# Encoder block on one core: weight norms two jobs ahead, table loads spread over a job, four eviction buffers, three transpose banks

## The chip, the cores and the metric

The program runs on one core of a Trainium2 chip. The metric is the device time of one launch in microseconds (us); for the kernel before it is the median of three runs. Everything about the program's inside comes from one profiled execution of it.

The core's engines have a queue of instructions each, which they work off in order: PE (TensorE) multiplies matrices into PSUM, DVE (VectorE) and ACT (ScalarE) do element-wise work, POOL (GpSimd) too, and SP (SyncE) issues nearly all DMAs of the stages told of here. Engines meet through semaphores. PSUM has eight banks of 128 x 512 fp32.

## The reference

One encoder layer on 2048 tokens of width 1024, in fp32. Cut to what matters here:

```python
h = rmsnorm(x, g_attn_norm)
proj = h @ w_in                       # 1024 -> 1952
q_a, k_a, v_a, c_q, c_kv, k_rope = split(proj, [512, 512, 512, 256, 128, 32])
out_a = mixer_dilated(q_a, k_a, v_a, rel_bias)   # 8 heads of 64, windows (128,1), (512,4), (2048,16)
out_b = mixer_mla(c_q, c_kv, k_rope, ...)        # latent attention
x = x + concat(rmsnorm(out_a), rmsnorm(out_b)) @ w_out
x = x + hierarchical_moe(rmsnorm(x), ...)
return rmsnorm(x, g_final)
```

`mixer_dilated` adds to every score a bias that depends on the distance of key and query (`rel_bias` through a bucket table).

## The kernel before

The code is scheduled by hand: on every engine the instructions stand in the order in which the Python code emits them. A projection in fp32 accuracy is made of three fp16 products: each operand is split into `hi` and `lo` (ACT writes `hi`, DVE the remainder `lo`), and 24 matmuls (8 blocks of the inner dimension x hi*hi, hi*lo, lo*hi) build one output tile. The scale of a split is a power of two taken from a norm of the weights: `pow2_scale` sums the squares over the partitions with a tiny matmul of ones (L375, called p2 below) and makes the power of two with some ten DVE instructions.

**The x stage** (0 to 150 us) runs over the 16 blocks of 128 tokens, c = 0 to 15. `stage_a` loads and normalises a block, `stage_b` transposes it on PE (L167, two tiles of one PSUM bank each from pool `pt`) and splits it out of PSUM (ACT L102, DVE L103) into `hT`, `stage_c` makes the latent projection of a block (24 matmuls of 416 columns, L176). Between them generators emit side work, a step for each c: `tables` makes the bias tables (pairs of matmuls L462/L463 into pool `tb`, copied out by DVE at L464, two banks), `vb_scale` and `vscale` take norms with p2 matmuls into `pt`.

**The jobs** (150 to 435 us): two "v" jobs of 16 chunks (24 matmuls of 256 columns, L336), then four "qk" jobs of 8 chunks (24 matmuls of 512 columns, L354). `jobs[i]` runs out of split weights; while it runs, the weights of job i+1 are split and those of job i+2 are fetched. At the start of job i, ahead of its first matmul, stands `qkscale(i + 1)`: an ACT square of the whole raw weight (`qk_junk`, L268), then two p2 matmuls. A chunk's PSUM tile (pool `pm`, four banks) is evicted by ACT L364 and DVE L365 into `qk_sb` (two buffers of each half), and SP stores both (L367). From job 2 on a generator `v_copies` (`vc`) makes SP issue DRAM-to-DRAM copies of v (`d_v`, `d_v1e`, `d_v4e`) after a chunk's matmuls, ahead of its store.

**The last job** runs two further things: `pre3` at its start loads what phase 3 needs first (`QA`, `KA`, `KB`, and the bias tables: `t16` in one DMA, `t1` in sixteen pieces, L500), and `ahead3` issues, one step for each chunk, five loads of v (L508) and then four pieces of the table `t4` (L518).

**Phase 3** is the dilated attention, head by head: S matmuls (L681/L682), bias added by POOL (`pp`, L723/L729), exponent by ACT and so on. POOL scales each bias table in place once (L614): `t16`, then `t1`, which needs all sixteen pieces; the first `pp` stands behind it.

The lines that set the order around a job:

```python
for i, (kind, g) in enumerate(jobs):
    if i == len(jobs) - 1:
        self.pre3(); a3 = self.ahead3()
    if i + 1 < len(jobs):
        if jobs[i + 1][0] == "qk":
            for _ in qkscale(i + 1): pass
        split_job(i + 1)
    if i + 2 < len(jobs): fetch(i + 2)
    # chunks: 24 matmuls; next(vc); next(a3); evict; store
```

## Time and profile before

| what | value |
| --- | --- |
| median of three runs | 2306.95 us (2306.91 to 2308.32) |
| the profiled execution's own time | 2312.83 us |
| its span, first to last instruction | 2310.6 us |
| mean granted TensorE clock | 0.953 |
| busy: PE | 2060.5 us (89% of the span) |
| busy: DVE, ACT, POOL | 1666.5 (72%), 1439.9 (62%), 1092.7 us (47%) |

The span is what the rows of the trace add up to; the profiled execution took 5.9 us more than the median run. A busy share is a mean over stages: PE is close to full over the whole, so what counts is where it stands idle and what it then waits for. A row of a timeline gives start and length in us, engine, line, operation, `out<-in`, shapes, how many instructions were run together, and in brackets the idle time just before with what ended it.

### The profile page before, as it was taken

To read this page: it belongs to the slowest core of one execution; us is meant where nothing else is said; L and a number is where in the kernel's file an instruction comes from. 1 tells how busy PE (TensorE), PEld (TensorE's weight loads), DVE (VectorE), ACT (ScalarE), POOL (GpSimd) and SP (SyncE) were. 2 spreads that over 40 slices of the span, in tenths; PEclk is the share of its full clock that TensorE was granted. 3 is DMA by queue.
4 is the path that set the end of the run, shared out by engine and by line. 5 is a ranking of instruction groups with operands and counts; after the bars stand their busy time and mean duration, and the time that the engine had idled before them with its cause. 6 is when DMAs were issued, how large, how long until landed. Compare 5 with 4: busy or idle time off the path is not lost. (4 is left out here: it accounts for less than half of the span.)

```text
span 2310.6 us, 42905 instructions
## 1 busy us (share of the span) xinstructions
PE 2060.5 (89%) x16099; PEld 1458.3 (63%) x16099; DVE 1666.5 (72%) x3741; ACT 1439.9 (62%) x2125; POOL 1092.7 (47%) x1193
## 2 busy tenths in 40 slices
PE   5889989788889899999999999898888899999990
PEld 3458434577778466665655655577776588788870
DVE  7732221488887788888888899968787577777765
ACT  5532211499997588888888878744343366667653
POOL 1110000377763255555555556644654656667740
PEclk9989989999999899999999999899998999999995
DMA  4412344956735100000000221154444789999978
GB/s 153 131 54 68 123 151 122 224 139 153 163 100 154 37 20 22 6 22 21 7 22 9 55 93 24 34 165 143 150 147 147 219 298 293 291 308 319 311 211 308
DMA packets 196676, 312.81 MB, mean 135 GB/s; under 512 B 64185, under 2 KB 149090, under 8 KB 183460
## 3 DMA queue, kind: packets, MB, share of 16 engines
q1 hardware_dynamic: 166420, 174.43, 26.4%
q0 software_dynamic: 29760, 134.85, 18.2%
q8 instruction: 127, 2.08, 0.4%
q14 instruction: 81, 0.66, 0.1%
q10 hardware_dynamic: 288, 0.79, 0.1%
HBM read 235.66 MB, written 101.25 MB: 146 GB/s over the span
## 5 line engine op out<-in xcount | busy, mean ns | idle before, releaser
L961 POOL TENSOR_TENSOR lo<-p,hi 128x512 f16<-128x512 f32 x256 | 343.0, 1344 | 295.5 <-ACT p L955 233.7
L954 ACT ACTIVATE hi<-S,mla_scale 128x1024 f16<-128x1024 f32 x256 | 285.5, 1115 | 135.0 <-PE S L949 133.4
L923 DVE TENSOR_REDUCE part<-M 128x1 f32<-128x512 f32 x512 | 340.4, 680 | 13.1 <-PE M L921 11.7
L955 ACT ACTIVATE p<-S,mla_scale 128x1024 f32<-128x1024 f32 x256 | 285.2, 1114 | 0.0
L960 DVE TENSOR_TENSOR lo<-p,hi 128x512 f16<-128x512 f32 x256 | 228.9, 895 | 12.1 <-ACT p L955 10.3
L983 PE MATMUL O<-VB,lo 128*128 128x65 f16 x2048 | 198.9, 194 | 6.8 <-DVE lo L960 4.3
L978 PEld LDWEIGHTS <-hi 128*128 128x128 f16 x2048 | 184.9, 98 | 27.0 <-issue 21.5
L978 PE MATMUL O<-VB,hi 128*128 128x129 f16 (+1 forms) x2048 | 198.9, 215 | 0.0
L983 PEld LDWEIGHTS <-lo 128*128 128x128 f16 x2048 | 177.7, 99 | 17.4 <-DVE lo L960 5.9
L729 POOL TENSOR_TENSOR pp<-sb,st 128x256 f32<-128x256 f32 (+1 forms) x256 | 142.9, 581 | 45.1 <-DVE st L706 32.9
L2117 DVE TENSOR_TENSOR s<-raw,s 128x1024 fp32r<-128x1024 f32 x120 | 140.2, 1221 | 17.1 <-ACT s L2115 16.0
L1425 PE MATMUL pm<-s,mT_hi 128*128 128x512 f32 x512 | 137.3, 415 | 3.8 <-ACT mT_hi L1410 3.8
L2074 PE MATMUL pd<-s,hT 128*128 128x512 f32 x540 | 138.2, 404 | 1.7 <-ACT hT L2061 1.7
L614 POOL TENSOR_SCALAR t<-t,a_scale 128x512 f32<-128x512 f32 (+1 forms) x12 | 16.1, 1354 | 261.3 <-DMA t<-d_r 245.2
L2161 POOL DMA_INDIRECT d_x<-o,rec x47 | 88.1, 1874 | 106.7 <-ACT s L2115 33.7
L365 DVE SCALAR_TENSOR_TENSOR qk_sb<-pm,wscale,qk_sb 128x512 f16<-128x512 f32 x32 | 24.0, 750 | 149.3 <-ACT qk_sb L364 149.3
L746 PE MATMUL PT<-ident,pp 128*128 128x128 f32 (+1 forms) x640 | 104.5, 287 | 25.6 <-ACT pp L733 24.0
L2115 ACT ACTIVATE s<-raw 128x1024 fp32r<-128x1024 f32 x120 | 118.2, 1049 | 12.8 <-DMA raw<-in_w_up,eidx 6.8
L733 ACT ACTIVATE pp<-pp,a_scale 128x512 f32<-128x512 f32 (+1 forms) x160 | 114.0, 713 | 11.2 <-POOL pp L729 9.5
L2074 PEld LDWEIGHTS pd<-s,hT 128*128 128x128 f32 x540 | 101.2, 188 | 30.1 <-issue 4.3
L364 ACT ACTIVATE qk_sb<-pm,wscale 128x512 f16<-128x512 f32 x32 | 22.0, 688 | 153.4 <-DMA d_qk<-qk_sb 76.8
L1425 PEld LDWEIGHTS pm<-s,mT_hi 128*128 128x128 f32 x512 | 98.8, 198 | 26.1 <-ACT mT_hi L1410 4.1
(511 smaller groups left out, 5963.7 us busy)
## 6 DMA issues: line engine op xcount, KB each, us to landing
x<-in_x SPq DMA_DIRECT2D x32, 512.0 KB
na<-d_na SPq DMA_DIRECT2D x48, 264.0 KB
d_qk<-qk_sb SPq DMA_DIRECT2D x64, 128.0 KB
d_x<-x SPq DMA_DIRECT2D x16, 512.0 KB
d_h<-h SPq DMA_DIRECT2D x16, 512.0 KB
y<-d_x SPq DMA_DIRECT2D x16, 512.0 KB
out<-y SPq DMA_DIRECT2D x16, 512.0 KB
d_q<-qs SPq DMA_DIRECT2D x16, 384.0 KB
```

Of the source, the lines that this page charges most:

```text
L729: nc.gpsimd.tensor_sub(dst, src, res[:, s0 + i, 65:66, None, None].to_broadcast([128, 2, na, nx // 2]))
L923: nc.vector.tensor_reduce(part[m][:, qt, kc:kc + 1], ps, axis=AX.X, op=ALU.max)
L954: nc.scalar.activation(hi, ps, AF.Exp, scale=es)
L955: nc.scalar.activation(p32, ps, AF.Exp, scale=es)
L960: nc.vector.tensor_sub(lo[:, :, 0:LV], p32[:, :, 0:LV], hi[:, :, 0:LV])
L961: nc.gpsimd.tensor_sub(lo[:, :, LV:512], p32[:, :, LV:512], hi[:, :, LV:512])
L978: nc.tensor.matmul(o[:, c0:c0 + own], hi[:, j, q], V[:, 0:own], start=(kt == 0 and qt == 0), stop=False, skip_group_check=True)
L983: nc.tensor.matmul(o[:, c0:c0 + 65], lo[:, j, q], V[:, 0:65], start=False, stop=(kt == 15 and qt == 3), skip_group_check=True)
L1425: nc.tensor.matmul(ps[half], mT[a][:, j], wo[b][j // 2][:, j % 2, 512 * half:512 * half + 512], start=(n == 0), stop=(n == 23))
L2074: self.nc.tensor.matmul(ps[:, half], hT[a][:, j], w[b][:, j, 512 * half:512 * half + 512], start=(n == 0), stop=(n == len(k) - 1))
L2115: nc.scalar.activation(hi, src, AF.Copy)
L2117: eng.tensor_sub(lo, src, hi)
```

## The change

- `wscale` and `qkscale` get a tile for each use (6 and 4 instead of 3 and 2).
- `pt` (transposes) gets a third PSUM bank, `pm` (projections) goes from four to three. In the x stage the p2 matmuls of `vb_scale` and `vscale` write into pool `tb`, whose two banks the tables use, instead of `pt`.
- `qkscale(i + 2)` runs in steps inside job i: in v jobs one step after the matmuls of each chunk from 8 on, in qk jobs two steps after each chunk from 4 on. `qkscale(i + 1)` at the job's start is gone.
- `qk_sb` gets four buffers instead of two.
- The sixteen `t1` loads leave `pre3`. `ahead3` issues two of them after each v load and ahead of each `t4` piece.

```diff
-            wsc = [hp.tile([128, 3], F32, name=f"wscale{i}") for i in range(3)]
-            sq = [hp.tile([128, 2], F32, name=f"qkscale{i}") for i in range(2)]
+            wsc = [hp.tile([128, 3], F32, name=f"wscale{i}") for i in range(6)]
+            sq = [hp.tile([128, 2], F32, name=f"qkscale{i}") for i in range(4)]
...
+            norms = []
...
-                yield from self.pow2_scale(sm, pt, am, 1.0, w[:, 0:1], None, w[:, 1:2])
+                yield from self.pow2_scale(sm, norms[0], am, 1.0, w[:, 0:1], None, w[:, 1:2])
...
-            pt = ctx.enter_context(tc.tile_pool(name="p1pt", bufs=2, space=PSUM))
-            pm = ctx.enter_context(tc.tile_pool(name="p1pm", bufs=4, space=PSUM))
+            pt = ctx.enter_context(tc.tile_pool(name="p1pt", bufs=3, space=PSUM))
+            pm = ctx.enter_context(tc.tile_pool(name="p1pm", bufs=3, space=PSUM))
...
-                yield from self.pow2_scale(sm, pt, am, float(D), vsc, dr["va_inv"])
+                yield from self.pow2_scale(sm, norms[0], am, float(D), vsc, dr["va_inv"])
...
                 nc.scalar.activation(jk, raws[i], AF.Square, accum_out=am[:, 0:1])
                 nc.vector.tensor_copy(am[:, 2:3], gmax)
-                s2 = sq[g % 2]
+                yield
+                s2 = sq[g]
...
             tb = c1.enter_context(tc.tile_pool(name="p1tb", bufs=2, space=PSUM))
+            norms[0] = tb
             tables = self.bias_tables(rawp, xp.tile([128, 4, 768], F32R, name="onehot", bufs=1), tb)
-            vb = self.vb_scale(rawp, pt, sm)
+            vb = self.vb_scale(rawp, tb, sm)
...
                 if c == NT - 1:
                     c1.close()
+                    norms[0] = pt
...
-                    if jobs[i + 1][0] == "qk":
-                        for _ in qkscale(i + 1):
-                            pass
                     split_job(i + 1)
+                steps = iter(())
                 if i + 2 < len(jobs):
                     fetch(i + 2)
+                    steps = qkscale(i + 2)
...
+                        if c >= 8:
+                            next(steps, None)
                         vt = vts[c % 2]
...
-                            s2 = wsc[g % 2 + 1][:, 2:3]
-                            qs = [qkp.tile([128, 512], F16, name=f"qk_sb{t}") for t in range(2)]
+                            if 4 * hh + n4 >= 4:
+                                next(steps, None)
+                                next(steps, None)
+                            s2 = wsc[g + 1][:, 2:3]
+                            qs = [qkp.tile([128, 512], F16, name=f"qk_sb{t}", bufs=4) for t in range(2)]
...
-        for c in range(16):
-            nc.sync.dma_start(self.t1[8 * c:8 * c + 8], AP(dr["t1"], (15 - c) * 16, [[496, 8], [8 * 496, 8], [1, 256]]))
...
+        def table1(c0):
+            for c in range(2 * c0, 2 * c0 + 2):
+                nc.sync.dma_start(self.t1[8 * c:8 * c + 8], AP(dr["t1"], (15 - c) * 16, [[496, 8], [8 * 496, 8], [1, 256]]))
...
-        yield from self.load_v(0, self.v_first)
+        for i, _ in enumerate(self.load_v(0, self.v_first)):
+            table1(i)
+            yield
         for a in range(4):
+            table1(4 + a)
             nc.sync.dma_start(self.t4[32 * a:32 * a + 32].rearrange("p h (a x) -> p (h a) x", a=4),
                               AP(dr["r4"], a * 3072, [[1, 32], [96, 32], [1, 64]]))
             yield
```

Three places show how the instructions stand. First ACT at the boundary from job 3 to job 4, before: evictions of job 3 (`qk_sb`, L364), then `qk_junk`, the square of the weights of job 5, and `wc_hi`, the split of those weights (the bracket names the semaphores that the instruction waits for, by engine or DMA queue):

```order
L364 ACTIVATE qk_sb_2828<-pm,wscale_114 128x512 [waits DMAHW0_49,DVE_49,PE_49]
L364 ACTIVATE qk_sb_2861<-pm,wscale_114 128x512 [waits DMAHW4_49,DVE_49,PE_49]
L364 ACTIVATE qk_sb_2894<-pm,wscale_114 128x512 [waits DMAHW0_49,DVE_49,PE_49]
L364 ACTIVATE qk_sb_2927<-pm,wscale_114 128x512 [waits DMAHW4_49,DVE_49,PE_49]
L364 ACTIVATE qk_sb_2959<-pm,wscale_114 128x512 [waits DMAHW0_49,DVE_49,PE_49]
L364 ACTIVATE qk_sb_2991<-pm,wscale_114 128x512 [waits DMAHW4_49,DVE_49,PE_49]
L268 ACTIVATE qk_junk,vmax<-raw 128x2048 [waits DMAHW5_49]
L102 ACTIVATE wc_hi<-raw,wscale_114 128x16x64 [waits DVE_49]
L102 ACTIVATE wc_hi<-raw,wscale_114 128x16x64
```

and with the change, all eight evictions of job 3 (L374), with the same weights' square and split:

```order
L374 ACTIVATE qk_sb_2767<-pm,wscale_114 128x512 [waits DMAHW2_49,PE_49,Activation_49]
L374 ACTIVATE qk_sb_2800<-pm,wscale_114 128x512 [waits DMAHW5_49,PE_49,Activation_49]
L374 ACTIVATE qk_sb_2833<-pm,wscale_114 128x512 [waits DMAHW7_49,DVE_49,PE_49]
L374 ACTIVATE qk_sb_2866<-pm,wscale_114 128x512 [waits DMAHW2_49,DVE_49,PE_49]
L271 ACTIVATE qk_junk,vmax<-raw 128x2048 [waits DMAHW5_49,DMAHW4_49]
L374 ACTIVATE qk_sb_2909<-pm,wscale_114 128x512 [waits DMAHW0_49,DVE_49,PE_49]
L374 ACTIVATE qk_sb_2956<-pm,wscale_114 128x512 [waits DMAHW4_49,DVE_49,PE_49]
L374 ACTIVATE qk_sb_3001<-pm,wscale_114 128x512 [waits DMAHW0_49,DVE_49,PE_49]
L374 ACTIVATE qk_sb_3033<-pm,wscale_114 128x512 [waits DMAHW4_49,DVE_49,PE_49]
L102 ACTIVATE wc_hi<-raw,wscale_116 128x16x64 [waits DVE_49]
L102 ACTIVATE wc_hi<-raw,wscale_116 128x16x64
```

The square has moved from the boundary up into the middle of job 3, behind the fourth of its evictions, so four evictions lie between it and the split that needs its norm.

Next SP at the start of the last job. `QA` to `KB` and `t_3300` (t16) are loaded by `pre3`, `t_3301` is t1, `v` the loads of `ahead3`, `d_qk<-qk_sb` the stores of chunks. Before:

```order
L367 DMA d_qk<-qk_sb_3283 128x512
L560 DMA QA_3302<-d_qk 64x2048 x2
L564 DMA KA<-d_qk 64x2048 x2
L564 DMA KB<-d_qk 64x2048 x2
L498 DMA t_3300<-d_r_67 128x8x128
L500 DMA t_3301<-d_t_65 8x8x256 x16
L508 DMA v_3353<-d_va 128x16x260
L367 DMA d_qk<-qk_sb_3355 128x512
L367 DMA d_qk<-qk_sb_3356 128x512
L508 DMA v_3353<-d_v_59 128x15x260
L508 DMA v_3353<-d_v1e 96x4x260
L367 DMA d_qk<-qk_sb_3388 128x512
```

and with the change (`t_3306` is t1):

```order
L377 DMA d_qk<-qk_sb_3288 128x512
L575 DMA QA_3307<-d_qk 64x2048 x2
L579 DMA KA<-d_qk 64x2048 x2
L579 DMA KB<-d_qk 64x2048 x2
L508 DMA t_3305<-d_r_67 128x8x128
L516 DMA v_3342<-d_va 128x16x260
L525 DMA t_3306<-d_t_65 8x8x256 x2
L377 DMA d_qk<-qk_sb_3346 128x512
L377 DMA d_qk<-qk_sb_3347 128x512
L516 DMA v_3342<-d_v_59 128x15x260
L516 DMA v_3342<-d_v1e 96x4x260
L525 DMA t_3306<-d_t_65 8x8x256 x2
```

The block of sixteen t1 loads ahead of the first v load is gone; two t1 loads stand behind each step of `ahead3`, and the first store moves up ahead of fourteen of them.

Last, PE in the x stage at c = 5: the transposes of the next block, the two tables of this step and the p2 matmul of `vb_scale` (`vbmax`), behind which stand the latent matmuls of the block. Before:

```order
L167 MATMUL pT<-ident,xn 128x128 [waits DVE_49]
L167 MATMUL pT<-ident,xn 128x128 x3
L167 MATMUL pT<-ident,xn 128x128 [waits DVE_49]
L167 MATMUL pT<-ident,xn 128x128 x3
L462 MATMUL pT<-onehot 8x496 [waits DVE_49]
L463 MATMUL pT<-onehot 8x496
L462 MATMUL pT<-onehot 8x496 [waits DVE_49]
L463 MATMUL pT<-onehot 8x496
L375 MATMUL pT<-vbmax,ones 128x2 [waits DVE_49]
```

and with the change:

```order
L169 MATMUL pT<-ident,xn 128x128 [waits PE_49]
L169 MATMUL pT<-ident,xn 128x128 x3
L169 MATMUL pT<-ident,xn 128x128 [waits DVE_49]
L169 MATMUL pT<-ident,xn 128x128 x3
L472 MATMUL pT<-onehot 8x496 [waits DVE_49]
L473 MATMUL pT<-onehot 8x496
L472 MATMUL pT<-onehot 8x496 [waits DVE_49]
L473 MATMUL pT<-onehot 8x496
L385 MATMUL pT<-vbmax,ones 128x2 [waits DVE_49,Activation_49]
```

The order of these is the same; the p2 matmul's tile now comes from the two banks of the tables, so it waits on DVE for the first table's copy (L464 before, L474 with the change).

## Rows read from the trace of the kernel before

**Rows 1.** What PE waited for in the x stage and the jobs, 0 to 450 us (line waited for: us in total, times, longest).

```profile
PE pT L375 <- ACT qk_junk L268: 16.1, 4, 8.6
...
PE pm L336 <- DVE w_lo L103: 0.8, 1, 0.8
```

**Rows 2.** Timeline of PE in the jobs: the first matmuls of job 0; the end of job 0 (eight 256-column matmuls in a row); the end of job 3, its boundary and the first matmuls of job 4; the first of job 5. The row at 288.44 is the first of job 3.

```profile
150.63 1.04 PE L336 MATMUL pm<-w_hi,hT_hi 128*128 128x256 f16 x8
...
191.79 1.04 PE L336 MATMUL pm<-w_lo,hT_hi 128*128 128x256 f16 x8
192.66 1.04 PE L336 MATMUL pm<-w_hi,hT_lo 128*128 128x256 f16 x8
...
288.44 3.57 PE L354 MATMUL pm<-hT_hi,wc_hi 128*128 128x512 f16 x8
...
329.08 1.89 PE L354 MATMUL pm<-hT_hi,wc_lo 128*128 128x512 f16 x8
330.80 1.89 PE L354 MATMUL pm<-hT_lo,wc_hi 128*128 128x512 f16 x8
341.26 1.01 PE L375 MATMUL pT<-vmax,ones 128*128 128x2 f32 x4 [8.56 <-ACT qk_junk L268]
342.13 3.31 PE L354 MATMUL pm<-hT_hi,w_hi 128*128 128x512 f16 x8
...
384.99 1.89 PE L354 MATMUL pm<-hT_hi,wc_hi 128*128 128x512 f16 x8
```

**Rows 3.** Timeline of ACT at the end of job 3 and in job 4.

```profile
322.49 0.69 ACT L364 ACTIVATE qk_sb<-pm,wscale 128x512 f16<-128x512 f32 x1 [4.61 <-DMA d_qk<-qk_sb]
...
338.63 0.69 ACT L364 ACTIVATE qk_sb<-pm,wscale 128x512 f16<-128x512 f32 x1 [7.39 <-DMA d_qk<-qk_sb]
339.21 1.90 ACT L268 ACTIVATE qk_junk<-raw 128x2048 bf16<-128x2048 f32 x1
...
370.83 1.38 ACT L364 ACTIVATE qk_sb<-pm,wscale 128x512 f16<-128x512 f32 x2 [7.36 <-DMA d_qk<-qk_sb]
```

**Rows 4.** Timeline of SP (DMA issue) in job 3: the stores of a chunk, and the copy behind them.

```profile
331.26 1.11 SPq L367 DMA_DIRECT2D d_qk<-qk_sb  x2
332.42 0.59 SPq L418 DMA_DIRECT2D d_v4e<-d_va  x1
```

**Rows 5.** Timeline of SP in job 5: the t1 loads, and the load behind them.

```profile
392.00 14.91 SPq L500 DMA_DIRECT2D t<-d_t  x15
407.62 0.39 SPq L508 DMA_DIRECT2D v<-d_va  x1
```

**Rows 6.** Timeline of ACT in job 5: the fourth eviction.

```profile
419.37 0.69 ACT L364 ACTIVATE qk_sb<-pm,wscale 128x512 f16<-128x512 f32 x1 [23.13 <-DMA d_qk<-qk_sb]
```

**Rows 7.** Timeline of PE in job 5 and at the start of phase 3.

```profile
420.89 3.18 PE L354 MATMUL pm<-hT_hi,wc_hi 128*128 128x512 f16 x8 [4.66 <-DVE qk_sb L365]
...
430.81 1.89 PE L354 MATMUL pm<-hT_lo,wc_hi 128*128 128x512 f16 x8
438.85 0.27 PE L681 MATMUL S<-KA,QA 128*128 128x128 f16 x1 [6.15 <-DVE qk_sb L365]
```

**Rows 8.** Timeline of POOL: the scaling of t1, and the first bias additions of phase 3.

```profile
416.04 1.56 POOL L614 TENSOR_SCALAR t<-t,a_scale 128x512 f32<-128x512 f32 x1 [16.13 <-DMA t<-d_t]
441.09 4.07 POOL L723 TENSOR_TENSOR pp<-sb,st 128x512 f32<-128x512 f32 x4 [23.48 <-DVE st L706]
```

**Rows 9.** DMA from 387 to 440 us: its busy tenths in 40 slices of 1.3 us.

```profile
DMA  4699999955556555899999999999999999978899
```

**Rows 10.** Busy time by stretch, 387 to 440 us: PE, PEld, DVE, ACT, POOL, granted clock, DMA share of 16 engines, GB/s.

```profile
387.00:440.00 53.00, 42.19 (x196) 19.27 (x195) 6.01 (x8) 6.62 (x11) 2.50 (x2) 0.94 0.98 192
```

**Rows 11.** Timeline of PE in the x stage: c = 5 and 6, then parts of c = 12, 13 and 14.

```profile
63.24 0.38 PE L375 MATMUL pT<-vbmax,ones 128*128 128x2 f32 x2 [0.18 <-DVE hT_lo L103]
...
67.70 0.60 PE L167 MATMUL pT<-ident,xn 128*128 128x128 f32 x4
70.88 0.66 PE L167 MATMUL pT<-ident,xn 128*128 128x128 f32 x4 [2.57 <-DVE hT_lo L103]
...
72.93 2.77 PE L176 MATMUL pm<-wc_hi,hT_hi 128*128 128x416 f16 x8
75.53 1.57 PE L176 MATMUL pm<-wc_hi,hT_lo 128*128 128x416 f16 x8
...
116.83 0.59 PE L375 MATMUL pT<-vmax,ones 128*128 128x2 f32 x2 [2.93 <-DVE hT_lo L103]
117.28 2.93 PE L176 MATMUL pm<-wc_hi,hT_hi 128*128 128x416 f16 x8
...
131.47 0.56 PE L375 MATMUL pT<-vmax,ones 128*128 128x2 f32 x2 [3.26 <-DVE vmax L107]
...
141.69 0.66 PE L167 MATMUL pT<-ident,xn 128*128 128x128 f32 x4 [2.57 <-DVE hT_lo L103]
```

**Rows 12.** Timeline of DVE in the x stage, c = 5 and 6: table copies (L464) and splits (L103).

```profile
67.42 1.24 DVE L464 COPY raw<-pT 8x496 f32<-8x496 f32 x2
70.07 0.75 DVE L103 SCALAR_TENSOR_TENSOR hT_lo<-pT,hscale,hT_hi 128x512 f16<-128x512 f32 x1 [1.41 <-ACT hT_hi L102]
72.29 0.75 DVE L103 SCALAR_TENSOR_TENSOR hT_lo<-pT,hscale,hT_hi 128x512 f16<-128x512 f32 x1 [1.47 <-ACT hT_hi L102]
...
76.83 1.24 DVE L464 COPY raw<-pT 8x496 f32<-8x496 f32 x2
```

More of the change, by code (lines that the diff above doesn't have):

```diff
@@ L179, in stage_c @@
                 cj = cev.tile([128, 256], BF16, name="c_junk")
-                o = wsc[2][:, 2:3]
+                o = wsc[5][:, 2:3]
                 nc.scalar.activation(cj, ps[:, 0:256], AF.Square, scale=o, accum_out=self.css[:, 0, c:c + 1])
@@ L193, in split_c @@
             def split_c(h):
-                split(wcv[0][:, 4 * h:4 * h + 4], wcv[1][:, 4 * h:4 * h + 4], wraw[h], wsc[2][:, 0:1])
+                split(wcv[0][:, 4 * h:4 * h + 4], wcv[1][:, 4 * h:4 * h + 4], wraw[h], wsc[5][:, 0:1])
                 cj = cev.tile([128, 256], BF16, name="c_junk")
@@ L197, in split_c @@
                                      accum_out=self.mam[:, 3 + h:4 + h])
+            norms.append(pt)
             am = sm.tile([128, 4], F32, name="vmax")
@@ L207, in phase1 @@
                 nc.scalar.activation(wcv[h][:, 0:4], wraw[h], AF.Square, accum_out=am[:, h:h + 1])
-            list(weight_scale(am, wsc[2], 1.0))
+            list(weight_scale(am, wsc[5], 1.0))
             split_c(0)
@@ L237, in split_job @@
                 r = raws.pop(i)
-                sc = wsc[0 if kind == "v" else g % 2 + 1][:, 0:1]
+                sc = wsc[0 if kind == "v" else g + 1][:, 0:1]
                 if kind == "v":
@@ L273, in qkscale @@
                 yield from self.pow2_scale(sm, pt, am, float(D), s2[:, 0:1], None, s2[:, 1:2], low=16.0)
-                yield from weight_scale(a2, wsc[g % 2 + 1], s2[:, 0:1])
+                yield from weight_scale(a2, wsc[g + 1], s2[:, 0:1])
                 a = self.asc[:, g]
@@ L460, in table @@
         def table(src, n, dst):
-            ps = psp.tile([128, 512], F32, name="pT")
+            ps = psp.tile([128, 4, 128], F32, name="pT").rearrange("p a b -> p (a b)")
             nc.tensor.matmul(ps[:8, :n], rbh, src, start=True, stop=False)
```

## The prediction

> **What bounds the kernel now.** I read the waits of PE first, because PE is close to full over the whole span. Up to 450 us, where every edit lies, the dearest wait is that of the p2 matmul for `qk_junk`: four times, 16.1 us together, once 8.6 [rows 1]. The timeline of PE then says what the boundaries cost in all. Job 0 starts at 150.63 and job 5 at 384.99, 234.4 us apart. Eight 256-column matmuls take 0.87 us and eight 512-column ones 1.72 (start to start [rows 2]), so two v jobs (2 x 16 x 3 x 0.87 = 83.8) and three qk jobs (3 x 8 x 3 x 1.72 = 124.2) need 208.0 us. So 26.3 us are lost: the 16.1 waited, 0.8 for `w_lo` at the start, four pairs of p2 (the last 0.87, from 341.26 to 342.13), and the rest slow matmuls behind a stall, as the eight that take 3.31 us instead of 1.89 at 342.13 [rows 2].
>
> The reader should see why the fourth boundary is the worst. ACT's evictions at the end of job 3 wait for their buffer's store, and `qk_junk` stands behind them: 338.63 for the eviction, 339.21 for the square, 341.26 for the p2 [rows 2, 3]. Those evictions come 8.05 us apart (322.49 to 338.63 is two, 338.63 to 370.83 four [rows 3]), since each store stands behind a DRAM copy on SP [rows 4], and a chunk needs only 5.18 us of PE. This chain ends 82.4 us after job 3 began (370.83 [rows 3] less 288.44 [rows 2]).
>
> In job 5 sixteen t1 loads occupy SP's queue from 391.4 to 407 us, 0.97 us each [rows 5]. The stores stand behind them, so ACT's fourth eviction is idle for 23.1 us until 419.37 [rows 6], PE waits 4.66 us for a PSUM bank, its last matmuls start at 430.81, and the first S matmul waits 6.15 us more for the last eviction [rows 7]. POOL had scaled t1 at 416.04 and starts the bias additions at 441.09 [rows 8]: 56.1 us after the start of job 5. From there phase 3 runs without such gaps, so I count a gain here by when this first addition starts.
>
> **Part A, norms ahead and deeper buffers.** The square of job i + 2 sits in the middle of job i, behind an eviction, and the p2 behind a chunk's matmuls, so at the boundary only the split is left, which is not new. In job 3 four evictions stand ahead of the square, and with four buffers these need only stores of job 2. All 26.3 us go but the 0.8 for `w_lo` and the p2 pairs themselves, which still run (0.87 with slow matmuls around it, about half at full rate, four times: 1.9): 23.6. What is late next is the copy chain, which the edit does not shorten. If it ends 82.4 us behind the start of job 3 again, and PE reaches job 5 after 2 x 41.4 = 82.9, then job 4's sixth chunk, whose buffer is freed by the store behind the last copy, is evicted at about 84 with 1.5 us for both halves; three banks let PE run two chunks beyond it, so the first chunk of job 5 waits. The bounds are 0 (the chain starts a few us earlier) and 4.6 (it starts when its chunk ends and pays every period); I take 2.5. **A = -21.1** (bounds -23.6 and -19).
>
> **Part B, job 5.** With the stores no longer behind sixteen loads and four buffers, PE runs its 41.4 us without a wait, and S, whose three banks are now those of the transposes, no longer needs the last eviction. If nothing else were late, the first S would start 41.5 us after the job's start, and POOL 2.2 to 3 later as before: at 44.5, 11.6 earlier. But POOL scales t1 first, and the last two pieces are now issued behind the seventh chunk's matmuls. The DMA engines moved 0.98 x 53 = 52.0 us of work between 387 and 440 [rows 10], and in the ten slices or so in which t1 was alone they were only half busy [rows 9]; from 406 on they are full. The same transfers are wanted again, all but the last t4 piece and store ahead of the last t1 piece. Started 2 us into the job and kept full they end at 50 to 54; with 1.6 us of scaling [rows 8] POOL starts at 52 to 56. I take 53: **B = -3**, with the bounds -11.6 (the DMA keeps up with issue) and +1.4 (57.5, a little idle DMA time between issues).
>
> The slices at 5 tenths are t1's own: sixteen loads of 64 KB with half the engines busy [rows 9]. The Trainium skill ("DMA: Bandwidth & Descriptors", "Why a DMA increments its semaphore by 16 and not by 1") says that a DMA of this kind uses as many engines as divide the slowest dimension of both sides, at most sixteen; eight rows would give eight engines, always the lowest, and the trace agrees with about half. By it t1 costs those eight engines 15.5 us wherever it is issued, which is the late end of my span, 54; if its loads spread over all sixteen it would be near 46.
>
> **Part C, the x stage.** Nothing of this is announced by the waits, it comes from the bank counts. At c = 5 the p2 of `vb_scale` ran at 63.24 [rows 11]. With the change it takes a bank of the tables and so waits for DVE's copy of the first table, which runs at 67.42 behind a split, a square-root chain and a scaling [rows 12]: the copy ends at 68.0, so PE stands 4.9 us. At c = 6 that bank is held still, and the second table waits for the copy of the first. That copy ran at 76.83 [rows 12], 6.76 behind the first split at 70.07, of which 1.47 was waiting that the third transpose bank takes away; the split starts 2.4 behind the transposes at 67.70. So copy end at 67.70 + 2.4 + 5.3 + 0.6, and the latent matmuls at 8.9 behind the transposes instead of 5.2 (72.93 less 67.70 [rows 11]): 3.7. After such a stall eight 416-column matmuls took 2.77 or 2.93 us, at full rate 1.57 [rows 11]; I add 1.8 and 0.6. Loss: 4.9 + 1.8 + 3.7 + 0.6 = 11.0, bounds 5 (DVE does the copies sooner since its splits no longer wait) and 14.
> The gain is at the end of the stage. At c = 12 the p2 no longer waits 2.93 for a transpose bank, and the slow latent matmuls behind it (two groups of eight at 2.93 instead of 1.57) go: 5.6. At c = 13 its second p2 still waits for DVE's scalar chain (3.26 [rows 11]), of which I give 1.6 back; at c = 14 2.57 for the bank goes [rows 11]; half a us before. 5.6 + 1.6 + 2.6 + 0.5 = 10.3. **C = +1**, bounds -5 and +4. The smaller edits (scale tiles, table tile shape) cost nothing: they add no instruction.
>
> **Sum.** -21.1 - 3 + 1 = -23.1 us of the span of 2310.6. The profiled execution itself took 2312.83; the median run is 5.9 shorter, and I take the same difference off it: 2306.95 - 23.1 = **2284 us**.
>
> **The rivals.** *Job 5 is free of DMA.* The t1 pieces are hidden and the first addition comes at 44.5: B = -11.6, sum -31.7, 2275 us. For it: half-empty DMA slices now filled. Against: DMA was at nine tenths in all slices from 406 us on [rows 9].
> *The waits move.* The copy chain holds job 5 back the full 4.6, t1 lands at 57.5 and the tables' banks cost their upper bound: -19 + 1.4 + 4 = -13.6, 2293 us. For it: the chain is unchanged, and its 8.05 us beat PE's 5.18. Against: three terms at their bounds together.
> *The edit does not take the stall away.* If the mid-job square lands behind an eviction that waits for a copy's store (7.4 us [rows 3]), PE stops mid-job instead of at the boundary; only the stalls of the first three boundaries go. That leaves about -10 for A, with +1 and -3: 2295.
> *Slower.* t1's last piece gates POOL's queue: stores, v, t4 and t1 in one order behind chunks. A and C together give 20, so it decides once the first addition starts more than 76 us after the start of job 5; then the 52 us of DMA work must take 74, the mean 192 GB/s [rows 10] must fall to 135, as in the slices when t1 ran alone. At 85 us the time would be 2316.
>
> **Chances.** Forecast 0.55, with its own range 2279 to 2289; DMA-free job 5 0.18; waits move 0.14; stall not taken 0.05; slower 0.04; no change, several of the losses at their bounds together, 0.04. A measurement tells apart about 0.2%, 4.6 us. All cases but the last two are faster by more: 0.92; same 0.04, slower 0.04. The range reaches from the DMA-free case to the moved waits: 2271 to 2295.
>
> **What would show it.** Right: no p2 wait on `qk_junk` at a boundary, jobs 0 to 4 back to back in about 211 us; new PE waits at c = 5 and c = 6 on DVE's table copy, about 5 and 7 us; no 23 us gap of ACT in job 5; S directly behind the last projection; POOL's wait for t1 ending 50 to 54 us into job 5. Wrong: the first bias addition far from 53 us into job 5 on either side, a stall of more than 5 us at job 5's start behind `qk_sb`, or phase 3 whose later heads wait longer for loads that used to be issued earlier.

## The result, and the profile after

| | before | with the change |
| --- | --- | --- |
| median, us | 2306.93 (2305.28 to 2308.32) | 2282.24 (2279.93 to 2288.02) |
| ratio | | 0.9898 (0.988 to 0.9915) |
| profiled execution: span, us | 2310.6 | 2280.7 |
| first matmul of job 0, us | 150.63 | 150.81 |
| from there to the first matmul of job 5 | 234.36 | 212.11 |
| from there to POOL's first bias addition | 56.10 | 51.39 |
| from there to the end of the span | 1869.5 | 1866.4 |

The change makes the kernel 1.0% faster, 24.7 us by the medians. The profiled executions lie 29.9 us apart, 26.8 of them ahead of the first bias addition; the last row is a stretch in which the two programs are alike, and in the other kernels below it came out between 1858.6 and 1869.7 us, so its 3.1 us say nothing of the change. Medians and ratios, here and below, are those of runs in the usual, fast state; one of the four runs of h1 took 2947.86 us at a granted clock of 0.651 and is left out.

What PE waits for up to 450 us, where [rows 1] had `qk_junk` with 16.1 us:

```profile
...
PE PT L761 <- ACT pp L748: 10.1, 7, 8.4
PE pT L472 <- DVE raw L474: 8.5, 3, 6.5
PE pT L385 <- DVE raw L474: 5.2, 1, 5.2
...
PE pm L361 <- DVE qk_sb L375: 1.7, 1, 1.7
```

The wait for `qk_junk` is not in the list any more. (The line left out at its head, 13.5 us for `wc_lo`, lies ahead of the first block and stood at 13.4 before.) In its place stand two waits for a table's copy by DVE (L474, the x stage), one of 1.7 us for an eviction, and at the start of phase 3 one for `pp`. The timeline of PE shows the jobs, where [rows 2] and [rows 7] stood before: the first matmul of job 0, the first of job 5, the last group of job 5, and the first transposes of phase 3.

```profile
150.81 1.04 PE L341 MATMUL pm<-w_hi,hT_hi 128*128 128x256 f16 x8
...
362.92 1.89 PE L361 MATMUL pm<-hT_hi,wc_hi 128*128 128x512 f16 x8 [1.70 <-DVE qk_sb L375]
...
402.63 1.89 PE L361 MATMUL pm<-hT_lo,wc_hi 128*128 128x512 f16 x8
...
416.16 1.12 PE L761 MATMUL PT<-ident,pp 128*128 128x128 f32 x4 [8.35 <-ACT pp L748]
```

Five jobs in 212.1 us, with one gap of 1.70 us in front of job 5. ACT's evictions in job 4, and the last one of job 5 (where [rows 3] and [rows 6] stood):

```profile
336.96 0.69 ACT L374 ACTIVATE qk_sb<-pm,wscale 128x512 f16<-128x512 f32 x1 [6.04 <-DMA d_qk<-qk_sb]
345.01 0.69 ACT L374 ACTIVATE qk_sb<-pm,wscale 128x512 f16<-128x512 f32 x1 [7.37 <-DMA d_qk<-qk_sb]
353.06 0.69 ACT L374 ACTIVATE qk_sb<-pm,wscale 128x512 f16<-128x512 f32 x1 [7.36 <-DMA d_qk<-qk_sb]
...
404.56 0.69 ACT L374 ACTIVATE qk_sb<-pm,wscale 128x512 f16<-128x512 f32 x1 [4.49 <-DMA t<-d_t]
```

The copy chain is still there, 8.05 us from one eviction to the next, and no longer stops PE until job 5's start. In job 5 no eviction waits for a store; the last comes right behind its matmuls. POOL's rows, where [rows 8] stood:

```profile
412.77 1.56 POOL L629 TENSOR_SCALAR t<-t,a_scale 128x512 f32<-128x512 f32 x1 [34.85 <-DMA d_qk<-qk_sb]
414.31 4.06 POOL L738 TENSOR_TENSOR pp<-sb,st 128x512 f32<-128x512 f32 x4
```

t1 was complete at 412.77, 49.85 us after job 5 began, and the additions begin 1.5 us later; the bracket names a store, but what the scaling needs is t1's last load, which SP issued at 406.88, ahead of a piece of `t4` and of the store of the last chunk. The DMA share in the last stretch up to there (columns as in [rows 10]):

```profile
360.00:413.00 53.00, 44.77 (x230) 21.03 (x228) 10.69 (x35) 9.07 (x14) 1.15 (x2) 0.96 1.00 215
```

Again a share of about one; the S matmuls had begun at 404.36, so the additions waited for t1 alone.

### The profile page after: what moved, and what is told of

Read it like the earlier page. It is cut to its first block, busy times and chain, and to the rows that moved or that the text cites. A ratio compares the mean times of both kernels' runs of the same rounds, so it can differ in the third digit from the quotient of the medians.

```text
span 2280.7 us, 42909 instructions
## 1 busy us (share of the span) xinstructions
PE 2046.7 (90%) x16099; PEld 1451.8 (64%) x16099; DVE 1659.5 (73%) x3741; ACT 1436.6 (63%) x2125; POOL 1097.3 (48%) x1193
## 5 line engine op out<-in xcount | busy, mean ns | idle before, releaser
L938 DVE TENSOR_REDUCE part<-M 128x1 f32<-128x512 f32 x512 | 340.4, 680 | 13.5 <-PE M L936 12.2
L629 POOL TENSOR_SCALAR t<-t,a_scale 128x512 f32<-128x512 f32 (+1 forms) x12 | 16.1, 1350 | 257.9 <-DMA t<-d_t 223.0
L778 DVE TENSOR_TENSOR plo<-PT,phi 128x512 f16<-128x512 f32 (+1 forms) x160 | 109.6, 685 | 2.7 <-ACT phi L772 2.7
```

What stands on the lines that cost most here:

```text
L938: nc.vector.tensor_reduce(part[m][:, qt, kc:kc + 1], ps, axis=AX.X, op=ALU.max)
```

## The experiments

None of the kernels leaves out any part of the block. The table gives, from each profiled execution, the first matmul of job 0, the stretch from there to job 5's first matmul, the time from there to the first bias addition, and the median with its ratio to the kernel before on the same chip. The e kernels, the f kernels, and h1 with the g kernels ran on three different chips, on which the kernel before took 2304.75, 2305.12 and 2304.32 us.

| kernel | job 0 | jobs 0 to 4 | to first addition | median, us | ratio (95%) |
| --- | --- | --- | --- | --- | --- |
| before | 150.63 | 234.36 | 56.10 | 2306.93 | |
| the change | 150.81 | 212.11 | 51.39 | 2282.24 | 0.9898 (0.988 to 0.9915) |
| e1, t1 first | 152.10 | 211.98 | 52.06 | 2281.18 | 0.9915 (0.9892 to 0.9937) |
| e2, two buffers | 151.92 | 222.02 | 51.24 | 2290.98 | 0.9949 (0.9933 to 0.9965) |
| e3, vb's p2 in `pt` | 134.97 | 212.29 | 51.28 | 2268.56 | 0.9839 (0.981 to 0.9868) |
| e4, norms at the boundary | 150.25 | 225.24 | 51.14 | 2296.30 | 0.9957 (0.994 to 0.9975) |
| f1, e3 + t1 by fours | 137.83 | 212.11 | 46.32 | 2258.54 | 0.9789 (0.9759 to 0.982) |
| f2, e3 + t1 by POOL | 136.46 | 215.60 | 44.45 | 2262.97 | 0.9812 (0.9787 to 0.9837) |
| f3, e3 + wide copies | 134.59 | 210.25 | 51.50 | 2263.50 | 0.9814 (0.9789 to 0.9838) |
| f4, f3 + two buffers | 136.71 | 210.25 | 49.89 | 2262.88 | 0.9808 (0.9783 to 0.9834) |
| h1, e3 + two transpose banks | 140.00 | 210.25 | 52.57 | 2269.97 | 0.9852 (0.983 to 0.9873) |
| g1, f1 + f3 | 135.10 | 210.25 | 44.82 | 2254.36 | 0.9786 (0.9766 to 0.9806) |
| g2, f2 + f3 | 136.54 | 210.26 | 44.45 | 2255.76 | 0.9786 (0.977 to 0.9803) |

The intervals of e2, e3 and e4 lie clear of the change's, and g1's and g2's of e3's. Those of f1 to f4 and of h1 overlap with e3's, so what is said of these rests on the milestones of one profiled execution each. The x stage is the same in e3, the f and the g kernels, and job 0 starts at 134.6 to 137.8 in them: differences of 3 us there mean nothing.

The first four undo or alter one part of the change each.

### e1: t1 ahead of everything again

```diff
+        for c in range(16):        # in pre3, behind t16
+            nc.sync.dma_start(self.t1[8 * c:8 * c + 8], AP(dr["t1"], (15 - c) * 16, ...))
...
-            table1(i)
...
-            table1(4 + a)
```

> The changed kernel, but all sixteen t1 loads stand at the start of job 5 again, ahead of the first v load. In the changed kernel the first bias addition of POOL started 51.4 us after the start of job 5 (414.31 less 362.92) and POOL's wait for t1 ended at 49.9. Theory A (t1's last piece alone gates phase 3): t1 lands at about 31 us as before, four buffers and three banks keep PE from stopping, the first S matmul starts at about 41.5 and the first addition at 44 to 46, so 5 to 7 us faster than the changed kernel by the trace (2275 to 2278). Theory B (the DMA work of the stage gates it, whatever stands first): the first addition starts earlier, but the v and t4 loads come later, PE, ACT or POOL wait for them within the next 30 us, and the time is within 3 us of the changed kernel. Theory C (spreading is what brought job 5's gain): stores behind the sixteen loads stop PE again for 5 us or more, first addition at 53 or later, 2 to 6 us slower.

The time is that of the change. POOL's rows (scaling of t1, first addition) and ACT's fifth and last eviction in job 5, which began at 364.08:

```profile
395.77 1.56 POOL L629 TENSOR_SCALAR t<-t,a_scale 128x512 f32<-128x512 f32 x1 [16.63 <-DMA t<-d_t]
416.14 4.07 POOL L738 TENSOR_TENSOR pp<-sb,st 128x512 f32<-128x512 f32 x4 [18.80 <-DVE st L721]
```

```profile
399.12 0.69 ACT L374 ACTIVATE qk_sb<-pm,wscale 128x512 f16<-128x512 f32 x1 [13.44 <-DMA d_qk<-qk_sb]
...
413.19 0.69 ACT L374 ACTIVATE qk_sb<-pm,wscale 128x512 f16<-128x512 f32 x1 [4.72 <-DMA d_qk<-qk_sb]
```

t1 was there at 31.7 us, as theory A had it, and PE never stopped (its last group started at 404.10). But the fifth eviction waited 13.4 us for a store that stood behind the t1 loads, and the last one came at 413.19. DVE works in order, and its first step of phase 3 (L721) stands behind its half of that eviction:

```profile
414.06 0.75 DVE L375 SCALAR_TENSOR_TENSOR qk_sb<-pm,wscale,qk_sb 128x512 f16<-128x512 f32 x1 [4.79 <-ACT qk_sb L374]
415.06 0.29 DVE L721 CUSTOM_DVE_ANT_0 sb<-S,t 128x128 f32<-128x128 f32 x1 [0.25 <-DMA d_qk<-qk_sb]
```

So A fell, and C too: the first addition starts at 52.1, by another gate. Spreading the loads bought nothing here that the other edits (four buffers, three transpose banks) had not bought already: either the table is late or the stores are. B's number came out, but whether the amount of DMA work is what makes one of the two late was left open; f1 asks that.

### e2: two eviction buffers

```diff
-                            qs = [qkp.tile([128, 512], F16, name=f"qk_sb{t}", bufs=4) for t in range(2)]
+                            qs = [qkp.tile([128, 512], F16, name=f"qk_sb{t}") for t in range(2)]
```

> The changed kernel with two qk_sb buffers instead of four. Theory A (the copy chain of 8.05 us a step needs the depth): in job 4 the evictions run two chunks closer to the chain, PE waits some 10 us more before job 5 begins, and the square in the middle of job 3 comes behind an eviction that waits for a copy; the stretch from job 0 to job 5, 212.1 us in the changed kernel, becomes 220 to 228, and stores in job 5 add 0 to 4 us: 8 to 18 us slower than the changed kernel, 2290 to 2300. Rival B (three PSUM banks absorb it, norms ahead did all the work): stretch within 3 us of 212, time within 3 us of the changed kernel.

Theory A holds: 222.0 us instead of 212.1, and 8.7 us by the medians. The first and the last of PE's waits in job 4, and the start of job 5:

```profile
339.41 1.89 PE L361 MATMUL pm<-hT_hi,w_hi 128*128 128x512 f16 x8 [2.71 <-DVE qk_sb L375]
...
363.58 1.89 PE L361 MATMUL pm<-hT_hi,w_hi 128*128 128x512 f16 x8 [2.73 <-DVE qk_sb L375]
...
373.94 1.89 PE L361 MATMUL pm<-hT_hi,wc_hi 128*128 128x512 f16 x8
```

Four waits, 9.2 us together, 8.05 us apart: PE now follows the copy chain. In job 5 evictions wait for stores again with two buffers (ACT is idle for up to 8.14 us where 4.49 is usual), but the first addition still comes at 51.2, since t1 is later than they are. So the four are worth about 10 us, and all of it in job 4.

### e3: the p2 of vb_scale back in the transposes' pool

```diff
-            vb = self.vb_scale(rawp, tb, sm)
+            vb = self.vb_scale(rawp, pt, sm)
```

> The changed kernel, but the p2 matmul of vb_scale writes into the transposes' pool (three banks) again instead of the tables' pool; the p2 matmuls of vscale stay in the tables' pool. In the changed kernel PE waits 5.15 us at 67.82 and 6.54 us at 82.08 for DVE's table copy and runs slow matmuls behind it. Theory A (the two waits come from the bank that p2 takes from the tables): both go, with the slow matmuls behind them, and job 0 starts 9 to 13 us earlier than 150.81; the whole is 9 to 13 us faster, 2269 to 2273. Rival B (DVE's chain bounds the stage): the transposes or the latent matmuls wait in their place, job 0 starts at most 3 us earlier, time within 3 us of the changed kernel.

Theory A, and more than it asked for: job 0 starts 15.8 us earlier. PE in the x stage with the change (transposes of a block, p2, and the tables at c = 6, with the latent matmuls behind each stall):

```profile
59.54 1.04 PE L169 MATMUL pT<-ident,xn 128*128 128x128 f32 x8
...
67.82 0.56 PE L385 MATMUL pT<-vbmax,ones 128*128 128x2 f32 x2 [5.15 <-DVE raw L474]
68.24 2.94 PE L178 MATMUL pm<-wc_hi,hT_hi 128*128 128x416 f16 x8
...
82.08 0.58 PE L472 MATMUL pT<-onehot 33*8 33x496 f32 x1 [6.54 <-DVE raw L474]
...
83.01 2.95 PE L178 MATMUL pm<-wc_hi,hT_hi 128*128 128x416 f16 x8
...
89.81 1.04 PE L169 MATMUL pT<-ident,xn 128*128 128x128 f32 x8
```

The eight matmuls at 68.24 take 2.94 us instead of 1.57 because the granted clock is 0.50 there, the lower of its two levels (1.2 of 2.4 GHz), right after PE has stood idle for 5.15 us (columns as in [rows 10]):

```profile
68.24:71.00 2.76, 2.76 (x10) 1.20 (x11) 0.01 (x1) 0.00 (x0) 0.00 (x0) 0.50 0.66 200
```

The same transposes of blocks 6 and 8 in the kernel before:

```profile
59.94 1.04 PE L167 MATMUL pT<-ident,xn 128*128 128x128 f32 x8
...
78.35 1.04 PE L167 MATMUL pT<-ident,xn 128*128 128x128 f32 x8
```

and in e3 (transposes of blocks 6 and 8, the p2 of `vb_scale`, and the start of job 0):

```profile
60.04 1.04 PE L169 MATMUL pT<-ident,xn 128*128 128x128 f32 x8
...
63.10 0.38 PE L385 MATMUL pT<-vbmax,ones 128*128 128x2 f32 x2
...
73.89 1.04 PE L169 MATMUL pT<-ident,xn 128*128 128x128 f32 x8
...
134.97 1.04 PE L341 MATMUL pm<-w_hi,hT_hi 128*128 128x256 f16 x8
```

Theory A had the time at 2269 to 2273; the median, 2268.56, lies just below. From block 6 to block 8 the kernel before took 18.4 us, the change 30.3, e3 13.9. So the p2 in the tables' banks cost 11.9 us against before, and e3 gains 4.6 over before as well, since with three banks the transposes at c = 6 wait no longer. My expectation had left those out. From block 8 to job 0 it is 72.3 before, 61.0 with the change and 61.1 in e3.

### e4: norms at the boundary

```diff
                 if i + 1 < len(jobs):
+                    if jobs[i + 1][0] == "qk":
+                        for _ in qkscale(i + 1):
+                            pass
                     split_job(i + 1)
...
-                    steps = qkscale(i + 2)
```

> The changed kernel, but the norms are taken at the boundary again (the norm of job i + 1's weights at the start of job i); four buffers, three banks and spread loads stay. Theory A (the place of the norm is the larger part of the gain): p2 waits for qk_junk at four boundaries, 3.1 + 4.8 + 6.3 us lost at the first three and 3 to 6 at the last, which no longer stands behind a delayed eviction; the wait of 1.7 us at job 5's start goes; the stretch from job 0 to job 5 is 225 to 231 us instead of 212.1, and the whole 13 to 19 us slower than the changed kernel, 2295 to 2301. Rival B (buffers were the larger part): stretch below 219, time within 7 us of the changed kernel.

225.2 us from job 0 to job 5, the lower end of theory A, and 14.1 us by the medians. The four waits are back (first and last):

```profile
195.77 0.61 PE L387 MATMUL pT<-vmax,ones 128*128 128x2 f32 x4 [2.45 <-ACT qk_junk L271]
...
331.90 0.61 PE L387 MATMUL pT<-vmax,ones 128*128 128x2 f32 x4 [2.67 <-ACT qk_junk L271]
```

The last is now 2.67 us instead of 8.56 [rows 2]. So of the 22.2 us that the jobs gained, 13.1 hang on the place of the norms (with four buffers), and 9.1 on the buffers and the banks (with norms at the boundary); e2 gave 9.9 for the buffers with norms ahead. The two parts hardly overlap.

### f1 and f2: where the t1 loads stand

Both are built on e3. In f1 the loads go out four behind each of the first four steps:

```diff
-            table1(i)
+            table1(2 * i)
+            table1(2 * i + 1)
             yield
         for a in range(4):
-            table1(4 + a)
```

> e3 (the p2 of vb_scale in the transposes' pool), and the t1 loads go out four behind each of the first four steps of ahead3, instead of two behind each of eight; the t4 loads come behind them. In e3 the first bias addition starts 51.3 us after the start of job 5 (398.54 less 347.26), right behind the scaling of t1. In e1, with all t1 loads first, t1 was there at 31.7 us, but the evictions then waited for stores and DVE's first step of phase 3 stood behind the last of them: 52.1. Theory A (the order of loads decides: t1 has to go ahead of t4, but not ahead of the stores): t1 lands at 33 to 40 us, no eviction waits, the first addition starts at 44 to 47 and the time is 4 to 7 us below e3: 2261 to 2265. Theory B (only the DMA work counts): the first addition starts earlier, but within the next 30 us PE, ACT or POOL wait for v or t4 by as much; time within 2 us of e3.

POOL (scaling of t1, first addition), and the first matmul of job 5:

```profile
393.18 1.56 POOL L629 TENSOR_SCALAR t<-t,a_scale 128x512 f32<-128x512 f32 x1 [28.27 <-DMA d_qk<-qk_sb]
396.26 4.06 POOL L738 TENSOR_TENSOR pp<-sb,st 128x512 f32<-128x512 f32 x4 [1.52 <-DVE st L721]
```

```profile
349.94 1.89 PE L361 MATMUL pm<-hT_hi,wc_hi 128*128 128x512 f16 x8 [1.70 <-DVE qk_sb L375]
```

t1 is there 43.2 us into job 5, DVE's first step is the later of the two by 1.5, and the first addition starts at 46.3, as theory A had it. Two of its details missed: t1 was to be there at 33 to 40 us, and no eviction was to wait, but the last two waited for stores (ACT is idle for 5.00 and 5.75 us ahead of them, 4.49 is usual), and DVE's first step stands behind the last of them. PE does not pay for the earlier start later; the wait for `pp` in front of the transposes, 8.35 us at its longest with the change, is 2.9. The DMA engines were as full as before (same columns as above):

```profile
350.00:393.00 43.00, 42.88 (x216) 20.09 (x216) 6.46 (x9) 5.08 (x8) 0.93 (x1) 1.00 1.02 214
```

So the amount of DMA work alone did not set the time of t1: ahead of t4 it comes 6.6 us earlier than in the change. By the medians f1 is 10.0 us below e3 (2258.54, where theory A had 2261 to 2265), 5 more than the first addition explains; by the trace the stretch behind it was the shortest of all (1858.6 us), in stages that are alike in all kernels. The intervals of f1 and e3 overlap, and what made this stretch short stays open.

In f2 POOL issues the sixteen loads:

```diff
+        for c in range(16):        # in pre3, behind t16
+            nc.gpsimd.dma_start(self.t1[8 * c:8 * c + 8], AP(dr["t1"], (15 - c) * 16, ...))
```

> e3, and all sixteen t1 loads are issued by POOL at the start of job 5, so SP's queue holds only v, t4 and stores. Theory A (SP's queue, where at most some eight DMAs were seen outstanding, is what makes t1 and the stores wait for one another): t1 lands before 40 us, no eviction waits, the first addition starts at 44 to 47 us after the start of job 5: 4 to 7 us below e3, 2261 to 2265. Theory B (the DMA engines are full, whatever queue a load is in): stores and v loads are slowed by as much, first addition at 50 to 53, time within 2 us of e3.

```profile
310.44 4.79 POOL L510 DMA_DIRECT2D t<-d_t  x8 [170.83 <-DMA d_v<-d_va]
...
365.71 2.48 POOL L629 TENSOR_SCALAR t<-t,a_scale 128x256 f32<-128x256 f32 x2 [38.23 <-DMA t<-d_r]
396.51 4.07 POOL L738 TENSOR_TENSOR pp<-sb,st 128x512 f32<-128x512 f32 x4 [28.32 <-DVE st L721]
```

The number is theory A's, 44.45 us, the reason is another: POOL, idle until then, issued the loads from 310.44 on, in job 4, up to 42 us ahead of job 5 (352.06). There they ran against the copies, behind which the evictions then came 8.2 to 9.9 us apart, and the jobs took 3.5 us longer. That the median, 2262.97, lies in theory A's 2261 to 2265 is therefore luck: 6.8 us gained at the first addition, 3.3 lost in the jobs.

### f3 and f4: the copies of v

f3 is e3 with the copies written so that the slowest dimension is 15, 32 or 24 long instead of 4; of the last two the step is cut into three and four DMAs:

```diff
-                                  AP(va, (128 * c + 4) * R, [[128 * R, 4], [8 * R, 15], [1, 8 * R]])
+                                  AP(va, (128 * c + 4) * R, [[8 * R, 15], [128 * R, 4], [1, 8 * R]])
...
-            nc.sync.dma_start(AP(v4e, e * 96 * R, [[24 * R, 4], [4 * 96 * R, 4], [1, 24 * R]]), ...)
+            for y in range(4):
+                nc.sync.dma_start(AP(v4e, (e * 96 + 24 * y) * R, [[R, 24], [4 * 96 * R, 4], [1, R]]), ...)
```

> e3, and the DRAM copies of v are written so that their slowest dimension has 15, 32 or 24 entries instead of 4 (more and smaller pieces, the same bytes). Theory A (a copy step takes 8.05 us because it runs on a quarter of the DMA engines): a step takes 2 to 5 us, the evictions of job 4 no longer come 8.05 us apart, the wait of 1.9 us at job 5's start goes; stretch from job 0 to job 5 210 to 211 instead of 212.3, and the time 1 to 3 us below e3: 2266 to 2268. Rival B (a copy is limited by DRAM or by its bytes): evictions still about 8 us apart, no change.

Two of ACT's evictions in job 4, and below them two of f4 (f3 with two buffers):

```profile
324.32 0.69 ACT L374 ACTIVATE qk_sb<-pm,wscale 128x512 f16<-128x512 f32 x1 [4.49 <-PE pm L361]
329.50 0.69 ACT L374 ACTIVATE qk_sb<-pm,wscale 128x512 f16<-128x512 f32 x1 [4.49 <-PE pm L361]
```

> f3 with two qk_sb buffers instead of four. With the old copies two buffers cost 9.9 us between job 0 and job 5 (e2: 222.0 instead of 212.1). Theory A (the buffers were needed only against the copy chain): with short copies the stretch is 210 to 213 and the time within 3 us of f3. Rival B (two buffers are too few in themselves): the stretch is 217 to 223 and the time 7 to 11 us above f3.

```profile
336.80 0.69 ACT L374 ACTIVATE qk_sb<-pm,wscale 128x512 f16<-128x512 f32 x1 [4.49 <-PE pm L361]
341.98 0.69 ACT L374 ACTIVATE qk_sb<-pm,wscale 128x512 f16<-128x512 f32 x1 [4.49 <-PE pm L361]
```

In both the evictions come 5.18 us apart, as the chunks do, and the stretch is 210.25 us: the gap in front of job 5 is gone, and with two buffers it does not come back. Theory A holds in both, though f3's median is 5.1 us below e3's, where the stretch explains 2 and theory A had 1 to 3. Up to job 5 the buffers were needed against the copies only. In job 5 the evictions of f4 still wait for stores (ACT idle for up to 8.08 us); it costs nothing because t1 is later (first addition at 49.89). Whether two buffers would do in g1, where t1 comes earlier, no run here shows. The same bytes, in more and smaller pieces with a longer slowest dimension, go through in less than a chunk's time. The Trainium skill ("DMA: Bandwidth & Descriptors", "Why a DMA increments its semaphore by 16 and not by 1") gives the reason that fits: such a DMA runs on as many engines as divide the slowest dimension of both sides, so 4 before, and 12 to 16 in f3. No row names the engines, but the DMA share agrees (columns as in [rows 10]; the change in the copy chain of job 4, then f3 with only the stores left):

```profile
322.00:361.00 39.00, 39.00 (x182) 17.68 (x181) 5.81 (x7) 4.01 (x6) 0.00 (x0) 1.00 0.33 135
```

```profile
320.00:340.00 20.00, 20.00 (x94) 9.11 (x93) 2.87 (x4) 2.20 (x4) 0.00 (x0) 1.00 0.16 54
```

Stores alone take 0.16 of the engines when a chunk is stored every 5.18 us, so 0.10 when it is every 8.05 (an estimate). That leaves 0.23 for the copies of the change, the time of a little under four of sixteen engines: about what four engines can do if they are busy for the whole chain. f3 changes the slowest dimension, the size of the pieces and the number of DMAs together. The number of DMAs by itself made no difference before: in e2 the evictions behind steps of two DMAs (`d_v`) and of one (`d_v4e`), of the same bytes, all come 8.04 to 8.08 us apart. The size of the pieces was not varied alone.

### h1: two banks for the transposes, on e3

```diff
-            pt = ctx.enter_context(tc.tile_pool(name="p1pt", bufs=3, space=PSUM))
-            pm = ctx.enter_context(tc.tile_pool(name="p1pm", bufs=3, space=PSUM))
+            pt = ctx.enter_context(tc.tile_pool(name="p1pt", bufs=2, space=PSUM))
+            pm = ctx.enter_context(tc.tile_pool(name="p1pm", bufs=4, space=PSUM))
```

> e3 with two banks for the transposes and four for the projections, as in the kernel before; the p2 matmuls of vscale stay in the tables' pool. Theory A (the third transpose bank is worth several us in the x stage): the second half of a transpose waits for the split of the one before again, 2.57 us and slow matmuls behind it at c = 6, 13 and 14 and in places between, and job 0 starts at 140 to 147 us instead of 134.6 to 137.8; the fourth projection bank takes the 1.9 us at job 5's start away; S waits for the last eviction, but t1 comes later still: 3 to 9 us above e3. Rival B (what helped in the x stage was only p2 leaving the transposes' pool): job 0 at 134 to 139, time within 3 us of e3.

```profile
59.70 1.04 PE L169 MATMUL pT<-ident,xn 128*128 128x128 f32 x8
...
70.63 0.66 PE L169 MATMUL pT<-ident,xn 128*128 128x128 f32 x4 [2.57 <-DVE hT_lo L103]
...
79.74 1.04 PE L169 MATMUL pT<-ident,xn 128*128 128x128 f32 x8
...
140.00 1.04 PE L341 MATMUL pm<-w_hi,hT_hi 128*128 128x256 f16 x8
```

Job 0 starts at 140.0, theory A's lower edge (134.6 to 137.8 in the kernels with three); the time, 1.4 us above e3, is rival B's. From block 6 to block 8 it takes 20.0 us instead of 13.9, with the wait of 2.57 us back; the same waits at c = 13 and 14, which theory A had, do not come; from block 8 to job 0 it is 60.3, no longer than with three banks. So the third bank is worth some 5 us, at c = 6 only, and the 11 us that the end of the x stage gained came from vscale's p2 leaving the transposes' pool. With four projection banks the gap in front of job 5 is gone too (210.25), with the slow copies as they were. The intervals of h1 and e3 overlap, so the 5 us stand in the trace only.

### g1 and g2: together

> f1 and f3 together: p2 of vb_scale in the transposes' pool, t1 loads four behind each of the first four steps, wide copies of v. If the two gains are independent, the stretch from job 0 to job 5 is 210.2 us as in f3 and the first bias addition starts 46.3 us after the start of job 5 as in f1: 2 us below f1 at the same start of job 0, 2254 to 2259. If wide copies leave the DMA engines no fuller, nothing of either is lost; a rival is that stores run late in job 5 (two evictions waited in f1) and give the 2 us back.

> f2 and f3 together: t1 loads on POOL's queue, wide copies. In f2 the first addition started 44.6 us after job 5's start, earlier than in f1, but the loads of POOL ran while the copy chain of job 4 was still on its way: its steps took up to 9.2 us and PE waited 5.0 us instead of 1.9 at job 5's start. With short copies that loss should go: stretch 210 to 211, first addition 44 to 46 us into job 5, 2253 to 2258. Rival: POOL's loads disturb the stores of job 4 also without the long copies, and the stretch stays above 213.

g1 is f1 with f3's copies. POOL's rows; job 5 began at 345.35:

```profile
387.03 1.57 POOL L630 TENSOR_SCALAR t<-t,a_scale 128x512 f32<-128x512 f32 x1 [26.94 <-DMA d_qk<-qk_sb]
390.17 2.06 POOL L739 TENSOR_TENSOR pp<-sb,st 128x512 f32<-128x512 f32 x2 [1.58 <-DVE st L722]
```

44.8 us after job 5's start, and 210.25 for the jobs: the gains add up. g2 (POOL's queue, wide copies) has 44.45 and 210.26, so the copies were what POOL's loads had disturbed. Both are faster than the change and the kernel before; g1 at 2254.36 us has a ratio of 0.9786 (0.9766 to 0.9806) against 0.9898 for the change. g1 and g2 can't be told apart.

## Why the prediction was right

The time came out 2 us from the forecast, and the three terms each within 2 us of theirs, two of them for reasons that need mending. That it is only 2 us is in part luck: the terms together measured -26.8, 3.7 more than their sum of -23.1, the medians moved by 24.7, and the stretch behind the terms varies by more than these differences. The last of the signs of being wrong, a phase 3 that pays for later loads, did not show: from the first addition on the kernel took 1866.4 us against 1869.5.

**A, the jobs: -22.2 measured, -21.1 predicted.** The accounting held: the floor of 210.8 that the working implies (234.4 less 23.6) shows as 210.25 in the five kernels without a gap, and the gap in front of job 5 was 1.9 us where 2.5 was taken (its bounds 0 and 4.6). What is late next was named rightly, the copy chain: the sixth chunk of job 4 is evicted at 361.40, 83.5 us after job 3 began (277.90), where about 84 was said. Shorter copies take the gap away (f3), and so does a fourth projection bank (h1), so it took both: slow copies, and a PE that three banks let run only two chunks beyond a late eviction, as the working had it.

**B, job 5: -4.7 measured, -3 predicted.** t1 complete at 49.85 us lies just ahead of the span of 50 to 54, and the first addition at 51.4 where 53 was taken. But the step that the DMA work sets that time ("the same transfers are wanted again") was right for this order of loads only: put ahead of t4, t1 comes at 43 us with the DMA as full (f1), and earlier still from a queue that can start in job 4 (f2). The rival in which job 5 is free of t1 gave 44.5 us for its first addition; f1, f2, g1 and g2 reach 44.5 to 46.3. In the change itself it did not come true, since the last two pieces of t1 stand on SP behind the store of the seventh chunk and behind three pieces of t4. That t1 is spread is not needed for the 4.7: with four buffers the old order would have been as good (e1, 52.1). Nor are the four buffers, where t1 is spread (e2, 51.2). Which of the other edits would be enough by itself was not tried.

**C, the x stage: +0.2 measured, +1 predicted.** A small difference of two large terms, and both held: -11.3 from block 8 to job 0, where 10.3 was taken, and +11.9 at c = 5 and 6, where 11.0 was. The waits are those that were named, 5.15 us for p2 and 6.54 for the second table, with slow matmuls behind them (2.94 and 2.95 us for eight, 1.57 at full rate), at a granted clock of 0.50. The mis-assigned part is inside the gain: I put 2.57 us at c = 14 down to the third bank; h1 shows that bank to be worth nothing there, where vscale's p2 had stood in its way, and some 5 us at c = 6.

Some readings in the working were off without moving the forecast. The products of the printed factors are 83.5 and 123.8, not 83.8 and 124.2. The eviction of job 5 that stood for 23.1 us [rows 6] is the third, not the fourth. The slices at five and six tenths are eight, from about 398 to 408 us, and of those behind them four are at seven or eight tenths [rows 9]. The engines moved 67 GB/s between 398 and 408 us; 134 is the mean from 391 on, with other loads in it, so the 135 of the rival in which the kernel is slower is not the rate of t1 alone.

The rivals that end worse did not come: no eviction waited for a copy's store ahead of the square in the middle of job 3 (the square of job 3 stands behind an eviction that needs a store of job 2), and POOL's queue was free again at 51.4 us, far from the 76 at which the gain would have been gone.

## What to carry to other kernels

A tile that waits for a slow reader should not share a small pool with work that comes round every step: here one tiny matmul moved into a pool of two banks cost 12 us against the kernel before, and two rows of the order, with the reader's place in its engine's queue, were enough to see it. Where a wait moves, ask what its cause is before adding depth: either two more buffers or a different shape of the DMA that made the stores late was enough to win some 10 us. Of loads that all have to fit into a full stretch, the one that is wanted first has to go ahead of those that are wanted later, which spreading them evenly does not do (f1), but not in one block ahead of the stores that buffers wait for (e1).

## What the runs showed of the hardware

The DRAM copies of 780 KB took 8.05 us a step with a slowest dimension of 4, with about a quarter of the DMA engines' time (0.23 of 16, an estimate from the shares above), and up to 9.9 where loads of t1 ran beside them (f2). With 24 or 32 entries in it, in three or four DMAs instead of one or two, a step took no more than the 5.18 us of a chunk. Behind a stall of PE of 5.15 us the granted clock was 0.50 for the next 2.8 us (68.24 to 71.00 with the change). Sixteen loads of 64 KB with eight entries in the slowest dimension left the engines at five to six tenths busy [rows 9]. A stretch of about 1865 us in which the programs are alike varied by 11 us among thirteen profiled executions, more than most of the steps studied here; only milestones inside the trace could tell those apart.
